# PEER feed-forward on one core: constants, index lists and gated Gelu values kept in PSUM as one operand of VectorE's steps, and one step per half for the index products

## The chip, the cores and the metric

One core of a Trainium2 chip runs the whole program in one launch. The time is the device time of that core in microseconds; the kernel before was run three times, and the median stands for it. Five engines matter: TensorE (PE, with its weight loads PEld), VectorE (DVE), ScalarE (ACT), GpSimd (POOL) and the queue of SyncE (SP), which issues the large transfers. Tiles lie in SBUF or in PSUM; in this kernel PE's results go to PSUM, and POOL's steps have all their operands in SBUF.

## The reference

A model of two blocks on 512 tokens of width 1024: gated linear attention, a convolutional feed-forward, grouped-query attention, the feed-forward again; then a mixer of an mLSTM and stick-breaking attention, a cross attention over 256 memory tokens, and PEER, a feed-forward that looks its experts up. PEER is all that the change touches:

```python
q = (xt @ wq).reshape(T, 8, 2, 128)                  # 8 heads, two halves of a product key
s = einsum('thpc,hpnc->thpn', q, subkeys)            # 128 sub-keys per half
s_top, i_top = top_k(s, 16)
cand = s_top[:, :, 0, :, None] + s_top[:, :, 1, None, :]
cand_idx = i_top[:, :, 0, :, None] * 128 + i_top[:, :, 1, None, :]
best, pos = top_k(cand.reshape(T, 8, 256), 16)
experts = take_along_axis(cand_idx.reshape(T, 8, 256), pos)
gates = softmax(best)
act = gelu(einsum('cd,ced->ce', x, u[experts])) * gates
y = einsum('ce,ced->cd', act, v[experts])            # 128 experts a token, of 16384
```

## The kernel before, in words

All matrix products run in three passes of rounded high and low parts (`mm3`, L188 to L190), so each operand is split: ACT rounds the high part, DVE or POOL subtracts it (for weights L115 and L118, where `lsplit` says which engine makes which tile's low part).

`peer` (from L1148) works in four stages.

- Projections: 16 query tiles. DVE takes the top 16 of each list (`top16`, L1179 to L1183). On the way the normalised tokens 128 to 511 are scaled (`xf`, L1209) and split (`xnh` by ACT, `xnl` by POOL, L1212).
- Routing, `route(t)` for 128 tokens (order 1, 2, 3, then 0): best 16 of 60 candidate sums per head, then per half a comparison of 128x2048 with the 16-element iota (L1279), eight products with the index list `tf`, one per head (L1282; POOL takes heads 1 and 5, DVE the six others), and a reduction (L1286). For tokens 0 to 127 the result is the index column `idx` (L1359).
- One-hots, `onehots(t)` for tokens 128 to 511: 32 steps of 4 tokens. Each makes two one-hot tiles by comparing with the 128-element iota `iot` in SBUF: the first on DVE (L1321) or, every third step, on POOL (L1319); the second on DVE with its gate (L1332), or on DVE and ACT (L1325, L1330). PE multiplies them into an `ax` PSUM tile (L1334), ACT moves it to `stage` (L1336). The stages of tokens 128 to 383 are flushed to DRAM (`Gd`, 16 transfers of 1 MB on SP), that of the last 128 tokens stays. Meanwhile `fill` makes 42 of the 128 "up" products ahead of time and stores their Gelu values in DRAM (`Hd`).
- The gate stretch: all 16384 experts densely for tokens 128 to 511, in 128 tiles of 128 experts. A list `mix` strings 86 fresh and 42 stored tiles evenly, so that two fresh ones are mostly followed by a stored one. For each tile `gate(j)` has Gelu values (fresh: 24 matmuls, Gelu by ACT at L1229 from PSUM to the SBUF tile `gel`; stored: `gst`, fetched), multiplies them by the gate matrix (DVE L1450 with the fetched `gm`, 128x256; L1451 with `stage`, 128x128), and splits them (`ah` by ACT L1454, `al` by DVE L1455). `down()` runs one tile behind: 18 matmuls of 512 columns with the "pv" weights into six PSUM tiles `Y`, which stay for the whole stretch. In the same stretch tokens 0 to 127 are done expert by expert: POOL gathers rows of u and v (L1411), DVE makes the dot product (L1419), ACT its Gelu (L1420), DVE multiplies by the gate (L1427) and adds the v row (L1428).

PSUM has eight tiles of 128x512: four named `mm`, four `ax`. A scheduler sets each engine's order from the program's dependencies; where two steps touch one tile, the order of the program holds.

## Time and profile before

| | |
|---|---|
| median of three runs | 3059.61 us (3058.24 to 3059.70) |
| span of the profiled execution | 3059.2 us, 0.4 under that median |
| PE busy | 2939.6 us (96%) |
| DVE busy | 2103.6 us (69%) |
| ACT, POOL busy | 1324.5 us (43%), 1237.5 us (40%) |
| PE's granted clock, mean | 0.990 |
| share of the span by what ended the chain of waits | PE 22%, DVE 5%, ACT 2%, DMA 1%; the rest shows no wait |

Busy time is the union of an engine's instructions; PE's matmuls overlap in the record, so a busy PE is one with work in it, and what it loses is read from its idle time and from the waits. PEER starts near 1660 us: projections until 1780, routing and one-hots until 2120, the gate stretch until 3052.

### The profile page before, as it was taken

How to read it: one execution, taken by the hardware profiler on the slowest of the kernel's cores; microseconds unless marked ns; L12 is line 12 of the kernel's file. 1: busy time of each engine (PE TensorE's matmuls, PEld its weight loads, DVE VectorE, ACT ScalarE, POOL GpSimd, SP SyncE). 2: the span in 40 equal slices, each digit the busy share in tenths (PEclk: the TensorE clock that was granted, in tenths of full speed). 3: DMA queues.
4: the chain of work that ended last, by engine and by line, in shares of the span. 5: the costliest groups of instructions: out<-in, count | busy, mean ns of one | idle time of the engine just before them, and what ended most of it. 6: DMA issues, size and time to landing. Idle time of an engine off the chain costs nothing. (4 is left out here: it accounts for less than half of the span.)

```text
span 3059.2 us, 38865 instructions
## 1 busy us (share of the span) xinstructions
PE 2939.6 (96%) x14251; PEld 2460.2 (80%) x14251; DVE 2103.6 (69%) x3665; ACT 1324.5 (43%) x2174; POOL 1237.5 (40%) x773
## 2 busy tenths in 40 slices
PE   8999999999999999999999989789999999999998
PEld 6778888788788887875888778788888888888887
DVE  4656554557664546448645789985888878888786
ACT  4454333356542335326444346655333333333333
POOL 3224322342332323105313446755555555555453
PEclk9999999999999999999999989999999999999999
DMA  4113333321223332321332335374888888888785
GB/s 137 58 49 104 95 92 97 103 91 35 76 90 97 97 97 91 97 62 35 109 98 80 93 103 159 114 221 168 285 299 300 297 300 297 306 294 289 286 293 191
DMA packets 166095, 472.90 MB, mean 155 GB/s; under 512 B 15368, under 2 KB 79240, under 8 KB 149520
## 3 DMA queue, kind: packets, MB, share of 16 engines
q1 hardware_dynamic: 135840, 322.73, 33.5%
q0 software_dynamic: 18432, 134.23, 11.2%
q10 hardware_dynamic: 11632, 13.46, 1.3%
q8 instruction: 112, 1.84, 0.2%
q14 instruction: 79, 0.65, 0.1%
HBM read 443.23 MB, written 27.13 MB: 154 GB/s over the span
## 5 line engine op out<-in xcount | busy, mean ns | idle before, releaser
L118 POOL TENSOR_TENSOR wl<-w,wh 128x1024 fp32r<-128x1024 f32 x242 | 611.1, 2526 | 903.6 <-ACT wh L115 778.8
L115 ACT ACTIVATE wh<-w 128x1024 fp32r<-128x1024 f32 (+1 forms) x530 | 559.1, 1055 | 794.3 <-PE mm L189 500.6
L188 PE MATMUL mm<-sh,wh 128*128 128x512 f32 (+1 forms) x1888 | 752.2, 399 | 8.3 <-ACT sh L219 6.7
L189 PE MATMUL mm<-sl,wh 128*128 128x512 f32 (+1 forms) x1888 | 750.9, 398 | 2.3 <-POOL sl L199 1.3
L190 PE MATMUL mm<-sh,wl 128*128 128x512 f32 (+1 forms) x1888 | 748.6, 397 | 0.2 <-DVE wl L118 0.2
L118 DVE TENSOR_TENSOR wl<-w,wh 128x1024 fp32r<-128x1024 f32 (+1 forms) x288 | 366.2, 1272 | 229.7 <-ACT wh L115 222.5
L188 PEld LDWEIGHTS mm<-sh,wh 128*128 128x128 f32 (+1 forms) x1888 | 354.7, 188 | 97.1 <-ACT sh L219 7.2
L189 PEld LDWEIGHTS mm<-sl,wh 128*128 128x128 f32 (+1 forms) x1888 | 354.6, 188 | 92.1 <-issue 3.6
L190 PEld LDWEIGHTS mm<-sh,wl 128*128 128x128 f32 (+1 forms) x1888 | 354.8, 188 | 85.2 <-issue 1.4
L188 PE MATMUL mm<-xnh,wh 128*128 128x384 f32 x1024 | 348.3, 340 | 1.4 <-ACT gel L1229 1.4
L190 PE MATMUL mm<-xnh,wl 128*128 128x384 f32 x1024 | 347.3, 339 | 1.6 <-DVE wl L118 1.6
L189 PE MATMUL mm<-xnl,wh 128*128 128x384 f32 x1024 | 346.1, 338 | 0.0
L188 PEld LDWEIGHTS mm<-xnh,wh 128*128 128x128 f32 x1024 | 194.0, 189 | 5.1 <-ACT gel L1229 1.7
L189 PEld LDWEIGHTS mm<-xnl,wh 128*128 128x128 f32 x1024 | 194.0, 189 | 3.3
L190 PEld LDWEIGHTS mm<-xnh,wl 128*128 128x128 f32 x1024 | 193.9, 189 | 2.6 <-DVE wl L118 2.5
L188 PE MATMUL mm<-wh,ah 128*128 128x512 f32 x384 | 154.2, 402 | 35.8 <-ACT ah L1454 35.8
L279 DVE TENSOR_TENSOR xT<-xT,mm 128x512 f32<-128x512 f32 x80 | 54.7, 686 | 171.8 <-PE mm L190 171.8
L190 PE MATMUL mm<-wh,al 128*128 128x512 f32 x384 | 154.1, 401 | 2.3 <-DVE al L1455 2.3
L1411 POOL DMA_INDIRECT xT<-in_uv_dram,idx x64 | 101.6, 1588 | 129.3 <-DVE xt L1428 80.1
L189 PE MATMUL mm<-wl,ah 128*128 128x512 f32 x384 | 152.4, 397 | 0.0
L1411 POOL DMA_INDIRECT uv<-in_uv_dram,idx x64 | 101.0, 1578 | 126.0 <-DVE xt L1428 79.0
L189 PE MATMUL ax<-wl,ah 128*128 128x512 f32 x384 | 150.3, 391 | 0.0
(452 smaller groups left out, 5110.3 us busy)
## 6 DMA issues: line engine op xcount, KB each, us to landing
w<-in_pu_dram SPq DMA_DIRECT2D x128, 512.0 KB, 4.5
w<-in_pv_dram SPq DMA_DIRECT2D x128, 512.0 KB, 4.0
w<-in_up_dram SPq DMA_DIRECT2D x88, 512.0 KB, 3.5
w<-in_down_dram SPq DMA_DIRECT2D x48, 512.0 KB, 3.5
Gd<-stage SPq DMA_DIRECT2D x16, 1024.0 KB, 8.8
gm<-Gd SPq DMA_DIRECT2D x128, 128.0 KB, 5.4
w<-in_pq_dram SPq DMA_DIRECT2D x16, 512.0 KB, 3.6
Hd<-gel ACTq DMA_DIRECT2D x42, 192.0 KB, 1.9
```

Of the source, the lines that this page charges most:

```text
L115: SC.activation(h[:, :n], w[:, :n], AF.Copy)
L118: ins = eng.tensor_tensor(l[:, :n], w[:, :n], h[:, :n].bitcast(F32), ALU.subtract)
L188: PE.matmul(ps, lhsT=lh, rhs=rh, start=start, stop=False)
L189: PE.matmul(ps, lhsT=lh, rhs=rl, start=False, stop=False)
L190: PE.matmul(ps, lhsT=ll, rhs=rh, start=False, stop=stop)
L279: V.tensor_tensor(xT[:, c], xT[:, c], ps, ALU.add)
L1411: G.indirect_dma_start(out=uv, out_offset=None, in_=A["uv"], in_offset=bass.IndirectOffsetOnAxis(ap=idx[:, k:k + 1], axis=0))
```

## The change

- `norm.finish(in_psum=True)` leaves the norm factor of PEER in its PSUM tile; `xf` is an `ax` PSUM tile, and its low part is made by DVE instead of POOL.
- One `ax` tile `cst` is taken for routing and one-hots. ACT copies both iotas into it, and `route` writes its index list into its other half (L1248). The comparisons of DVE (L1284, L1325, L1329, L1336) and the index products read it there. POOL's own one-hots still read `iot` in SBUF.
- The eight index products of a half are one DVE step (L1287).
- Gelu values of the gate stretch stay in PSUM: `gate(j)` takes in turn an `mm` and an `ax` tile (`Y` holds three of each), Gelu works in place, a stored tile is copied into it by ACT (L1459), DVE multiplies in place (L1460, L1461), and ACT and DVE split it from there (L1464, L1465).
- The dot's value is multiplied by its gate on ACT (`SC.activation(d, d, AF.Copy, scale=...)`) instead of on DVE.

```diff
-        def finish(self, bc=True, col=False):
+        def finish(self, bc=True, col=False, in_psum=False):
-                self.rstd = main.tile([P, S], F32, name="rstd", tag="rstd", bufs=1)[:, :n]
+                self.rstd = ps if in_psum else main.tile([P, S], F32, name="rstd", tag="rstd", bufs=1)[:, :n]
...
-                xf = q_("xf", (P, TD), bufs=2)
+                xf = axps()[:, :TD]
-                G.tensor_tensor(xnl[:, c], xf, xnh[:, c].bitcast(F32), ALU.subtract)
+                V.tensor_tensor(xnl[:, c], xf, xnh[:, c].bitcast(F32), ALU.subtract)
...
+        cst = axps()
+        SC.activation(cst[:, 0:P], iot, AF.Copy)
+        SC.activation(cst[:, P:P + 16], iota, AF.Copy)
+        iotp, iotap, tfp = cst[:, 0:P], cst[:, P:P + 16], cst[:, 256:512]
...
-            tf = r_("tf", (P, 16, 16))
-            V.tensor_copy(tf, ti[t])
+            V.tensor_copy(tfp.rearrange("p (a b) -> p a b", b=16), ti[t])
+            tf = tfp.rearrange("p (h f k) -> p h f k", f=2, k=16)
...
-                for h in range(8):
-                    (G if h % 4 == 1 else V).tensor_tensor(oh[:, h * 16:(h + 1) * 16], oh[:, h * 16:(h + 1) * 16],
-                                    tf[:, 2 * h + half].rearrange("p (o i) -> p o i", o=1)
-                                    .to_broadcast([P, 16, 16]), ALU.mult)
+                o4 = oh.rearrange("p (h k) i -> p h k i", k=16)
+                V.tensor_tensor(o4, o4, tf[:, :, half].rearrange("p h (o i) -> p h o i", o=1)
+                                .to_broadcast([P, 8, 16, 16]), ALU.mult)
...
-            io4 = iot.rearrange("p (o i) -> p o i", o=1).to_broadcast([P, 4, P])
+            io4 = iotp.rearrange("p (o i) -> p o i", o=1).to_broadcast([P, 4, P])
...
-                        V.tensor_scalar(oh2[:, k], iot, rt[:, 1, tk:tk + 1], rt[:, 2, tk:tk + 1],
+                        V.tensor_scalar(oh2[:, k], iotp, rt[:, 1, tk:tk + 1], rt[:, 2, tk:tk + 1],
...
             SC.activation(d, d, AF.Gelu)
+            SC.activation(d, d, AF.Copy, scale=gate0[:, k:k + 1])
...
-                V.tensor_tensor(d, d, gate0[:, k:k + 1], ALU.mult)
...
-            gm, g = fetched.pop(j)
-            if g is None:
-                g = up(j)
+            gm, st = fetched.pop(j)
+            g = (mmps, axps)[turn[0] % 2]()[:, :TD]
+            turn[0] += 1
+            if st is None:
+                up(j, g)
+                SC.activation(g, g, AF.Gelu)
+            else:
+                SC.activation(g, st, AF.Copy)
             V.tensor_tensor(g[:, :2 * P], g[:, :2 * P], gm, ALU.mult)
```

How the order of DVE's instructions moves is seen at two places. The first is the end of routing. Before, the last part of `route(0)` stands between two one-hot stages: the index products (`oh` with `tf`), the reductions `e0` and `e1` and `idx` come ahead of the first comparisons of the last one-hots (`oh1`, `oh2`).

```order
L1279 TENSOR_TENSOR oh_17195<-fj_17165,iota_12802 128x2048
L1294 RECIPROCAL sm_17209<-sm_17209 128x8
L1282 TENSOR_TENSOR oh_17195<-oh_17195,tf_17113 128x256 x6
L1295 TENSOR_TENSOR gate0_12797<-gate0_12797,sm_17209 128x128
L1286 TENSOR_REDUCE e1_17205<-oh_17195 128x128
L118 TENSOR_TENSOR wl_16105<-w_15996,wh_16104 128x1024
L1358 SCALAR_TENSOR_TENSOR e0_17193<-e0_17193,e1_17205 128x128
L1359 CAST idx_12796<-e0_17193 128x128
L118 TENSOR_TENSOR wl_16175<-w_16066,wh_16174 128x1024
L1321 TENSOR_TENSOR oh1_16349<-rt_16345,iot_12804 128x512
L1325 TENSOR_TENSOR oh2_16351<-rt_16345,iot_12804 128x512
```

With the change they follow the last one-hots, directly ahead of the first tile's gate products; `ax_13859` is `cst`.

```order
L1329 TENSOR_TENSOR oh2_16972<-rt_16302,ax_13859 128x512
L1336 TENSOR_SCALAR oh2_16990<-ax_13859,rt_16302 128x128 x4
L1248 CAST ax_13859<-ti0_12810 128x256
L1284 TENSOR_TENSOR oh_17139<-fi_17120,ax_13859 128x2048
L1287 TENSOR_TENSOR oh_17139<-oh_17139,ax_13859 128x2048
L1290 TENSOR_REDUCE e0_17142<-oh_17139 128x128
L118 TENSOR_TENSOR wl_17232<-w_16906,wh_17231 128x1024
L1284 TENSOR_TENSOR oh_17144<-fj_17121,ax_13859 128x2048
L1287 TENSOR_TENSOR oh_17144<-oh_17144,ax_13859 128x2048
L1290 TENSOR_REDUCE e1_17147<-oh_17144 128x128
L1362 SCALAR_TENSOR_TENSOR e0_17142<-e0_17142,e1_17147 128x128
L1363 CAST idx_12796<-e0_17142 128x128
```

Moved are the write of the index list (L1248) and all that reads it, behind the last step that compares with `cst`. The lists of tokens 256 to 511 are written behind the one-hots of the tokens before them in the same way.

The second place is in the gate stretch, a fresh tile followed by a stored one. Before (`gel` fresh, `gst` stored, `scr` and `xt0` the dot step of tokens 0 to 127, `wl` a weight's low part):

```order
L118 TENSOR_TENSOR wl_20679<-w_20530,wh_20678 128x1024
L1450 TENSOR_TENSOR gel_20707<-gel_20707,gm_20561 128x256
L1451 TENSOR_TENSOR gel_20707<-gel_20707,stage_16348 128x128
L1455 TENSOR_TENSOR al_20712<-gel_20707,ah_20711 128x384
L1419 SCALAR_TENSOR_TENSOR scr_20740,dot_20739<-xT_67,xn_17240 128x1024
L1427 TENSOR_TENSOR dot_20667<-dot_20667,gate0_12797 128x1
L1455 TENSOR_TENSOR al_20751<-gst_20602,ah_20750 128x384
L1428 SCALAR_TENSOR_TENSOR xt0_17227<-uv1_17273,dot_20667,xt0_17227 128x1024
L118 TENSOR_TENSOR wl_20757<-w_20604,wh_20756 128x1024
```

With the change (`mm` the fresh tile, `ax` the stored one):

```order
L118 TENSOR_TENSOR wl_20474<-w_20327,wh_20473 128x1024
L1460 TENSOR_TENSOR mm_20433<-mm_20433,gm_20317 128x256
L1461 TENSOR_TENSOR mm_20433<-mm_20433,stage_16305 128x128
L1465 TENSOR_TENSOR al_20468<-mm_20433,ah_20467 128x384
L1423 SCALAR_TENSOR_TENSOR scr_20496,dot_20495<-xT_67,xn_17182 128x1024
L1432 SCALAR_TENSOR_TENSOR xt0_17169<-xT_67,dot_20424,xt0_17169 128x1024
L1465 TENSOR_TENSOR al_20509<-ax_20504,ah_20508 128x384
L1423 SCALAR_TENSOR_TENSOR scr_20537,dot_20536<-uv0_17214,xn_17182 128x1024
L1432 SCALAR_TENSOR_TENSOR xt0_17169<-xT_67,dot_20495,xt0_17169 128x1024
L118 TENSOR_TENSOR wl_20551<-w_20400,wh_20550 128x1024
```

The sequence is the same around the gate products; the step L1427 is gone from DVE, and in place of `gel` and `gst` the operands are `mm` and `ax`, that is, PSUM.

## Rows read from the trace of the kernel before

**Rows 1.** Busy time by stage: us, busy us of each engine (instructions), granted clock, DMA share, GB/s:

```profile
1660.00:1780.00 120.00, 118.10 (x580) 96.54 (x579) 89.94 (x524) 44.48 (x68) 51.12 (x27) 1.00 0.31 87
1780.00:2120.00 340.00, 291.52 (x1831) 278.95 (x1830) 296.23 (x785) 207.84 (x427) 209.38 (x182) 0.94 0.48 148
2120.00:3052.00 932.00, 893.67 (x4342) 786.02 (x4341) 769.72 (x1007) 334.88 (x570) 479.90 (x232) 0.99 0.80 288
```

**Rows 2.** Waits, 2110 to 3060: engine, tile and line, releaser, us, times, longest:

```profile
PE mm L188 <- ACT ah L1454: 35.8, 24, 3.7
...
PE mm L190 <- DVE al L1455: 2.3, 1, 2.3
```

**Rows 3.** Timeline of DVE: start, us, instruction, idle before it:

```profile
2432.19 3.22 DVE L1450 TENSOR_TENSOR gel<-gel,gm 128x256 f32<-128x256 f32 x1 [0.31 <-ACT gel L1229]
2435.34 0.28 DVE L1451 TENSOR_TENSOR gel<-gel,stage 128x128 f32<-128x128 f32 x1
```

**Rows 4.** Timeline of POOL, the same stretch:

```profile
2431.02 1.69 POOL L1411 DMA_INDIRECT xT<-in_uv_dram,idx  x1 [4.51 <-PE mm L190]
2432.73 2.40 POOL L118 TENSOR_TENSOR wl<-w,wh 128x1024 fp32r<-128x1024 f32 x1
```

**Rows 5.** Timeline of ACT, the same stretch:

```profile
2431.69 0.47 ACT L1229 ACTIVATE gel<-mm 128x384 f32<-128x384 f32 x1
2435.71 0.52 ACT L1454 ACTIVATE ah<-gel 128x384 fp32r<-128x384 f32 x1 [3.55 <-DVE gel L1451]
```

**Rows 6.** Timeline of PE, the same stretch:

```profile
2436.29 0.51 PE L188 MATMUL mm<-wh,ah 128*128 128x512 f32 x1 [1.38 <-ACT ah L1454]
```

**Rows 7.** Lines L1450, L1451: duration ns least/median/most, first and last start:

```profile
L1450 DVE TENSOR_TENSOR gel<-gel,gm x86: 412/420/3241, 2119.5 to 3041.1; 128x256 f32<-128x256 f32 x86
L1451 DVE TENSOR_TENSOR gel<-gel,stage x86: 275/283/3167, 2121.7 to 3041.4; 128x128 f32<-128x128 f32 x86
```

**Rows 8.** Line L279:

```profile
L279 DVE TENSOR_TENSOR xT<-xT,mm x80: 674/687/690, 227.1 to 1664.3; 128x512 f32<-128x512 f32 x80
```

**Rows 9.** Groups by line and shape, 1660 to 2120: busy us, mean ns, idle before:

```profile
L1332 DVE TENSOR_SCALAR oh<-iot,rt 128x128 f32<-128x128 f32 x252 | 84.6, 395 | 4.0 <-PE ax L1334 4.0
...
L1321 DVE TENSOR_TENSOR oh<-rt,iot 128x512 f32<-128x512 f32 x63 | 51.8, 822 | 20.0 <-ACT rt L1305 10.1 <-PE ax L1334 9.7
...
L1282 DVE TENSOR_TENSOR oh<-oh,tf 128x256 f32<-128x256 f32 x48 | 34.1, 745 | 0.0
L1325 DVE TENSOR_TENSOR oh<-rt,iot 128x512 f32<-128x512 f32 x33 | 27.8, 842 | 0.0
...
L1279 DVE TENSOR_TENSOR oh<-fj,iota 128x2048 f32<-128x2048 f32 x4 | 9.1, 2285 | 0.0
```

**Rows 10.** Lines L1332, L1321, L1282: ns least/median/most:

```profile
L1332 DVE TENSOR_SCALAR oh<-iot,rt x252: 329/336/2422, 1818.9 to 2097.1; 128x128 f32<-128x128 f32 x126
L1321 DVE TENSOR_TENSOR oh<-rt,iot x63: 668/679/2876, 1817.7 to 2093.1; 128x512 f32<-128x512 f32 x63
L1282 DVE TENSOR_TENSOR oh<-oh,tf x48: 405/415/2630, 1797.0 to 2016.3; 128x256 f32<-128x256 f32 x48
```

**Rows 11.** Lines L888 (source in PSUM) and L1264 (in SBUF):

```profile
L888 DVE TENSOR_SCALAR W<-ax,colt x16: 342/343/351, 1292.4 to 1368.6; 128x128 f32<-128x128 f32 x16
L1264 DVE TENSOR_SCALAR pi<-bi x8: 215/219/315, 1790.3 to 1995.3; 128x128 uint32<-128x128 uint32 x8
```

**Rows 12.** Busy time in pieces: flush gaps, one-hots, the seam behind them:

```profile
1880.00:1930.00 50.00, 39.73 (x229) 39.05 (x227) 48.80 (x130) 20.41 (x27) 26.04 (x17) 0.96 0.95 293
1930.00:1995.00 65.00, 56.38 (x366) 52.21 (x367) 63.62 (x191) 50.06 (x116) 47.60 (x46) 0.93 0.19 60
1995.00:2033.00 38.00, 36.99 (x213) 36.33 (x212) 28.77 (x38) 16.08 (x22) 13.90 (x9) 1.00 1.04 308
2033.00:2100.00 67.00, 57.28 (x387) 54.31 (x388) 56.28 (x117) 51.97 (x119) 50.85 (x51) 0.95 0.34 110
2100.00:2120.00 20.00, 18.60 (x128) 18.25 (x127) 4.34 (x5) 7.06 (x11) 8.02 (x5) 1.00 0.62 202
```

More of the change, by code (lines that the diff above doesn't have):

```diff
@@ L1194, in peer @@
             if i == 0:
-                norm.finish(bc=True, col=True)
+                norm.finish(bc=True, col=True, in_psum=True)
                 V.tensor_copy(rcol, norm.col)
@@ L1220, in peer, with up @@
         hp = rctx.enter_context(tc.tile_pool(name="hp", bufs=1, side="right", reuse_waits="tile"))
-        def up(j):
+        def up(j, ps):
             uh, ul = weight("pu", j)
-            ps = mmps()[:, :TD]
             for c in range(8):
@@ L1227, in up, with up_store @@
                 mm3(ps, uh[:, s], ul[:, s], xnh[:, c], xnl[:, c], c == 0, c == 7)
+        def up_store(j):
+            ps = mmps()[:, :TD]
+            up(j, ps)
             g = hp.tile([P, TD], F32, name="gel", tag="gel", bufs=3)
             SC.activation(g, ps, AF.Gelu)
-            return g
-        def up_store(j):
-            nc.scalar.dma_start(Hd[j], up(j))
+            nc.scalar.dma_start(Hd[j], g)
         ahead = deque(range(NA))
@@ L1279, in route @@
                 V.tensor_tensor(oh, pf.rearrange("p h (k o) -> p (h k) o", o=1).to_broadcast([P, P, 16]),
-                                iota.rearrange("p (o i) -> p o i", o=1).to_broadcast([P, P, 16]), ALU.is_equal)
-                for h in range(8):
-                    (G if h % 4 == 1 else V).tensor_tensor(oh[:, h * 16:(h + 1) * 16], oh[:, h * 16:(h + 1) * 16],
-                                    tf[:, 2 * h + half].rearrange("p (o i) -> p o i", o=1)
-                                    .to_broadcast([P, 16, 16]), ALU.mult)
+                                iotap.rearrange("p (o i) -> p o i", o=1).to_broadcast([P, P, 16]), ALU.is_equal)
+                o4 = oh.rearrange("p (h k) i -> p h k i", k=16)
+                V.tensor_tensor(o4, o4, tf[:, :, half].rearrange("p h (o i) -> p h o i", o=1)
+                                .to_broadcast([P, 8, 16, 16]), ALU.mult)
                 e = r_(f"e{half}", (P, P), bufs=2)
@@ L1435, in peer @@
         fetched = {}
+        turn = [0]
         def fetch(j):
```

## Prediction

> **What bounds the kernel now.** I read the busy table by stage first [rows 1]. TensorE (PE) is the bound nearly everywhere, but not equally. While the product-key queries are projected (1660 to 1780 us) it is busy 118.1 of 120 us: nothing that the change does there can show. While lists are routed and one-hots are built (1780 to 2120) it is busy 291.5 of 340 us and VectorE (DVE) 296.2: 48 us of PE's time stand open, and DVE is the fuller engine. In the gate stretch (2120 to 3052) PE is busy 893.7 of 932 us, DVE 769.7: 38 us stand open. These two stretches are all that the change can win from.
>
> Next come the waits of the gate stretch. PE's idle time has one name: 35.8 us in 24 waits of the first product for `ah`, and 2.3 us for `al` [rows 2]. To see what is late I follow one of them in the order of time. ScalarE (ACT) starts Gelu at 2431.69 [rows 5], DVE starts the product with `gm` (L1450) at 2432.19, and that step, of 128x256, takes 3.22 us [rows 3], where its median is 0.420 [rows 7]. Meanwhile GpSimd (POOL) gathers until 2432.71 and then splits a weight until 2435.13 [rows 4]; DVE's step ends 0.3 us after that. `ah` starts at 2435.71 [rows 5], PE at 2436.29 after 1.38 us idle [rows 6]. So a DVE step whose two inputs lie in SBUF, started beside a POOL step, lasts until POOL is done. Both gate products show it in their maxima: 3.24 us against 0.41, and 3.17 against 0.28 [rows 7]. The counter-example is L279, which adds a PSUM tile to an SBUF tile: all 80 lie between 0.674 and 0.690 us [rows 8], though POOL splits weights in that part of the program as well.
>
> The Trainium skill says the same (SBUF — State Buffer, section Who interferes with whom): VectorE with two SBUF inputs shares a read port with a GpSimd instruction that reads SBUF, the second to issue is blocked for the whole of the first, and with at most one SBUF input there is no contention outside the doubled modes. The 3.22 us and L279's narrow spread agree with it.
>
> **The change, part by part.**
>
> *Gate values in PSUM.* The two gate products get one PSUM input and one SBUF input; so does the subtraction that makes `al`. If L279 is the pattern, the 3 us cases go. What then remains of a gate: Gelu begins at 2431.69 and PE could have taken the product at 2436.29 - 1.38 = 2434.91, so 3.2 us are there. The undisturbed chain is about 0.5 (Gelu, from 2431.69 to 2432.19) + 0.42 + 0.28 + the hand-over to `ah` and from `ah` to PE, 0.09 + 0.58 (2435.62 to 2435.71, and on to 2436.29): 1.9 us, slack 1.3. The second product now waits for the first one; before, its start overlapped the end of the first by 0.07 [rows 3], and a hand-over is 0.09, so some 0.15 us per tile, inside the slack. ACT copies 42 stored tiles into PSUM: some 0.5 us each, 21 us on an engine that is busy 335 of 932 us [rows 1]; such a copy waits until a tile's buffer comes free, and a weight split queued behind it on ACT waits too, by less than a DVE step. Multiplying the dot value by its gate goes from DVE to ACT, 128 one-column steps; neither engine is the bound. No row shows DVE or ACT writing PSUM. Bounds: from nothing to what would use up the 1.3 us; I take nothing: L279 reads PSUM and shows no wait [rows 8], and it is the nearest row. Of the 38.1 us I take 36 as gone, with 2 left to starts of stretches. Ends: 20 (if every second POOL step now catches another DVE step that stands ahead of a gate) and 42 (matmuls also restart slowly after each of the 24 waits: 0.51 us in the row of rows 6).
>
> *One step for index products.* Per half, six DVE steps and two POOL steps become one DVE step of 128x2048. DVE's 48 steps are 34.1 us of busy time [rows 9], their mean 0.745 us against a median of 0.415 [rows 10]: POOL's own two stand beside them. The new step's nearest row is L1279, 128x2048, 2.28 us [rows 9]: 8 x 2.28 = 18.3. DVE saves 15.9 us, three quarters of it, 12, in the routes of tokens 128 to 511, which lie on the path; route(0) is seen below.
>
> *Constants in PSUM.* L1321 and L1325 compare two SBUF operands: 63 at a mean of 0.822 and 33 at 0.842 us [rows 9] against a median of 0.679 [rows 10]: 96 x 0.15 = 14 us of waiting for POOL's own one-hots, which goes. L1332 has one tensor operand: mean 0.395 [rows 9], median 0.336 [rows 10], so 252 x 0.059 = 15 us to win. Against it stands the price of PSUM as the source: L888, a 128x128 step of the same kind out of PSUM, takes 0.343 us, while L1264 out of SBUF takes 0.219 [rows 11]. So L1332 lands between 0.343 (+2 us over the 252) and 0.336 + 0.124 = 0.46 (+31); I take the middle, 0.40, +16, because L888 carries one pointer and L1332 two. Net 0; ends -13 and +16.
>
> The Trainium skill has a rule that speaks against this part (VectorE: DVE Perf Modes, section Why PSUM operands drop a tier): a one-source 32-bit step runs at double rate only out of SBUF. By that rule the 252 steps would be slower than now and the middle value would be right; by L888 alone, whose 0.343 is close to 0.336, the sum would be 13 us better.
>
> *What it does to the path.* DVE is busy 48.8 of 50, 63.6 of 65 and 56.3 of 67 us in the pieces where I say that it decides [rows 12], so 12 + 14 = 26 us less DVE work shortens the stretch by as much, if nothing else is late next. Two things could be. PE is busy 56.4 of 65 and 57.3 of 67 in the one-hot pieces [rows 12], so such a piece can shrink by 9 at most, three of them by 27 if the first is like the others. And the 16 flushes keep the DMA engines full, 0.95 and 1.04 of their time, in both gaps [rows 12]; a stage tile cannot be overwritten before its flush is read. In the second gap DVE already idles (28.8 of 38): there is nothing to win there, and the moved products of route(3), which now follow the one-hots of the tile before, find room. I take 26; ends +10 and -45 (all 48 us of PE's open time but 3).
>
> *What moves.* Index lists and iota lie in one tile, so a list can only be written after the one-hots that read that tile. For route(0) this puts six passes of 128x2048 (13.7 us) behind the last one-hots instead of into the flush gap. There, 2100 to 2120, DVE is busy 4.3 us and PE 18.6 with stored tiles and transposes [rows 12]: PE covers them. If it did not, up to 14 us come back. One of four `ax` buffers is pinned, leaving three for one-hot products; ACT empties one while PE fills another, so I cost it at nothing; without that cover, it is in the +10.
>
> *Projection stage.* Eight subtractions move from POOL to DVE, which is busy 89.9 of 120 us while PE is full [rows 1]: nothing.
>
> **Sum.** The profiled span is 3059.2 us, 0.4 below the median of the runs, 3059.6. 0 - 26 - 36 = -62: **2998 us** by the median. 0.2%, 6 us, is about what a measurement here can tell from no change.
>
> **The rivals.** (1) *Only the gate stretch gains.* The flush gaps and PE's own work set the one-hot stretch, DVE only fills time. For it: DMA at 0.95 to 1.04 in the gaps; against it: DVE idles for 1.2 and 1.4 us only in two of the pieces [rows 12]. 3059.6 - 36 = 3024.
>
> (2) *The block moves to a neighbour.* A weight split on DVE (L118) and the dot step after the gate still have two SBUF inputs, and stand before the next gate in DVE's queue; DVE had only 0.31 us to spare before the gate [rows 3]. A POOL step of 2.4 us that meets such a neighbour delays the gate by up to 2.1. If that keeps half of the waits: 3059.6 - 18 - 26 = 3016.
>
> The Trainium skill's page SBUF — State Buffer, in the same section, gives this rival its reason: what counts is who issues first, not which step it is.
>
> (3) *The change does not do what it says*: steps in place in PSUM are stretched beside POOL as before, because the other operand still comes from SBUF. Then only the joined index products win, and the moved ones give some back: 3059.6 - 12 + 12 = 3060. L279's spread speaks against it.
>
> (4) *Slower.* Writing PSUM is dear, the one price that no row shows. Gelu, both products and the stored copies write PSUM. From 1.3 us extra per gate on, the second of each pair of fresh tiles (43 of them) holds PE up; at 2.7 us extra the 62 us are eaten up (43 x 1.4 = 60), and at 3.4 us the kernel ends at 2998 + 43 x 2.1 = 3088. It would need these steps, 1.2 us together, to take nearly four times as long.
>
> **How the numbers follow.** Forecast 0.57; rival 1 0.13; rival 2 0.15; rival 3 0.05; rival 4 0.07; 0.03 for a loss by several small things at the seams. Faster by over 0.2%: 0.86 (the first three, with a hundredth for mixtures); within 0.2%: 0.05; slower: 0.09. The range takes in the forecast's bounds (route stretch -45, gate stretch -42, not both in full) and reaches past rivals 1 and 2: 2968 to 3042.
>
> **What would show it.** After the change the maxima of both gate products (L1460, L1461) should lie under 0.6 us, and PE's waits for `ah` in the gate stretch be under 6 us in all. The one-hot comparisons L1325 and L1329 should have means within 3% of their medians; L1336 shows the price of PSUM as source: near 0.34 or near 0.40. L1287 should take about 2.3 us. The one-hot pieces should be near 57 us each, PE-bound. It is wrong if the dot steps, L118 or the 3.2 us cases stand right ahead of late gates (rival 2), if the flush gaps have not moved while DVE idles more (rival 1), or if Gelu into PSUM takes well over 0.5 us (rival 4).

## The result, and the profile after

| | before | with the change |
|---|---|---|
| median | 3058.93 us (3055.99 to 3059.70) | 2979.97 us (2974.41 to 2980.35) |
| ratio | | 0.9739, 95% interval 0.9725 to 0.9752 |
| span of the profiled execution | 3059.2 us | 2972.1 us |

The change made the kernel 79 us faster; 62 were forecast, and the time lies inside the range. The profiled execution of the changed kernel was its fastest (2974.41 us), so the two profiles lie 87 us apart, 8 more than the medians. One profiled execution, that of e6 below, ran at a mean granted clock of 0.566 and took 4709 us, so e6 is given by the median of its four others and has no profile here. For a table by stage I cut both at the same marks: the last query product (L1201), the first `al` of the gate stretch, and the last output step. First and last starts are in these rows of single lines, of the kernel before

```profile
L1201 PE MATMUL ax<-sk,q x128: 270/275/377, 1672.2 to 1774.8; 128*128 128x128 f32 x128
L1455 DVE TENSOR_TENSOR al<-gel,ah x86: 557/558/2967, 2122.6 to 3042.4; 128x384 fp32r<-128x384 f32 x86
L1386 DVE SCALAR_TENSOR_TENSOR uv<-ax,fst,fb x3: 740/743/751, 3050.7 to 3054.7; 128x512 f32<-128x512 f32 x3
```

and of the changed one:

```profile
L1201 PE MATMUL ax<-sk,q x128: 272/275/377, 1669.4 to 1769.7; 128*128 128x128 f32 x128
L1465 DVE TENSOR_TENSOR al<-mm,ah x64: 543/557/559, 2083.8 to 2949.3; 128x384 fp32r<-128x384 f32 x64
L1390 DVE SCALAR_TENSOR_TENSOR uv<-ax,fst,fb x3: 740/743/749, 2963.6 to 2967.6; 128x512 f32<-128x512 f32 x3
```

| stage | before | with the change | difference | forecast |
|---|---|---|---|---|
| to the last query product | 1774.8 | 1769.7 | -5.1 | 0 |
| routing and one-hots, to the first `al` | 347.8 | 314.1 | -33.7 | -26 |
| gate stretch, to the last output | 932.1 | 883.8 | -48.3 | -36 |

Of the 5.1, 2.7 lie ahead of the projections, where nothing was changed, and 2.4 in them (e7). Both other stages gave more than forecast, in about the same proportion. A few of the 33.7 may be scatter: the profiles of e1, e10 and e11, whose routing and one-hots are the changed kernel's, have 315.5 to 318.6 us for it.

The stage that lost 33.7 us can be cut further, at the first and the last one-hot product of each 128 tokens (PE's L1334, with the change L1338). The "flush gaps" are the two pieces between the one-hots of two token tiles:

| piece | before | with the change |
|---|---|---|
| last query product to first one-hot | 45.2 | 41.6 |
| one-hots, tokens 128 to 255 | 59.5 | 55.7 |
| first flush gap | 51.3 | 36.9 |
| one-hots, tokens 256 to 383 | 63.9 | 59.1 |
| second flush gap | 42.0 | 43.0 |
| one-hots, tokens 384 to 511 | 62.4 | 57.7 |
| seam, to the first `al` | 23.5 | 20.0 |

The first flush gap alone gave 14.4 us, the three one-hot pieces 13.3 together. Busy time in the two flush gaps, columns as in [rows 1], before

```profile
1879.50:1930.80 51.30, 40.25 (x233) 39.58 (x232) 50.10 (x134) 21.08 (x29) 26.84 (x18) 0.95 0.93 287
1994.70:2036.70 42.00, 37.29 (x215) 36.62 (x214) 32.74 (x44) 16.50 (x24) 17.60 (x11) 0.98 1.05 311
```

and with the change:

```profile
1867.10:1904.00 36.90, 31.49 (x169) 30.32 (x168) 33.08 (x103) 13.14 (x22) 7.95 (x7) 0.91 1.02 306
1963.00:2006.10 43.10, 37.08 (x213) 35.78 (x211) 40.60 (x135) 20.31 (x29) 13.04 (x9) 0.98 1.03 313
```

Part of a route moved from the first gap, where DVE was full, to the second, where it had idled. Before, the last route for the one-hots (`route(3)`) made its list at 1900.8 us and its first reduction at 1923.8, in the first gap; with the change its list is written at 1961.6, behind the one-hots that read `cst`, and both its reductions end by 1987.5, in the second gap.

In the gate stretch the signs asked for are there. The gate products, formerly [rows 7], in the rows of their lines (least/median/most, ns):

```profile
L1460 DVE TENSOR_TENSOR mm<-mm,gm x64: 418/426/433, 2079.6 to 2941.1; 128x256 f32<-128x256 f32 x64
L1460 DVE TENSOR_TENSOR ax<-ax,gm x64: 418/425/433, 2084.2 to 2953.9; 128x256 f32<-128x256 f32 x64
L1461 DVE TENSOR_TENSOR mm<-mm,stage x64: 298/299/300, 2080.1 to 2941.5; 128x128 f32<-128x128 f32 x64
```

The longest of 128 is 0.433 us where it was 3.241. All waits of PE of the gate stretch by tile and line, from 2070 on, formerly [rows 2]:

```profile
PE mm L190 <- DVE al L1465: 2.6, 1, 2.6
PE ax L1405 <- ACT xt L1399: 1.9, 1, 1.9
PE mm L188 <- ACT ah L1464: 1.7, 2, 1.0
```

24 waits for `ah` of 35.8 us have become two of 1.7. The same situation as in [rows 3 to 6], a weight split on POOL beside a gate product, now reads so, in the timelines of POOL and of DVE:

```profile
2412.13 2.40 POOL L118 TENSOR_TENSOR wl<-w,wh 128x1024 fp32r<-128x1024 f32 x1 [0.44 <-ACT wh L115]
```

```profile
2412.46 0.43 DVE L1460 TENSOR_TENSOR mm<-mm,gm 128x256 f32<-128x256 f32 x1 [1.59 <-ACT mm L1457]
2412.93 0.30 DVE L1461 TENSOR_TENSOR mm<-mm,stage 128x128 f32<-128x128 f32 x1
2413.85 0.56 DVE L1465 TENSOR_TENSOR al<-mm,ah 128x384 fp32r<-128x384 f32 x1 [0.62 <-ACT ah L1464]
```

All three DVE steps run inside POOL's 2.40 us, none longer than elsewhere. The rows of the routing and one-hot stage, formerly [rows 9, 10], by line:

```profile
L1325 DVE TENSOR_TENSOR oh<-rt,ax x63: 671/686/690, 1809.5 to 2058.7; 128x512 f32<-128x512 f32 x63
L1329 DVE TENSOR_TENSOR oh<-rt,ax x33: 674/680/683, 1810.1 to 2059.3; 128x512 f32<-128x512 f32 x33
L1336 DVE TENSOR_SCALAR oh<-ax,rt x252: 396/401/411, 1810.7 to 2060.9; 128x128 f32<-128x128 f32 x126
L1287 DVE TENSOR_TENSOR oh<-oh,ax x8: 2267/2275/2287, 1793.3 to 2073.2; 128x2048 f32<-128x2048 f32 x8
```

No comparison is stretched any more, and the one-hot pieces of 55.7, 59.1 and 57.7 us lie near the 57 that were named as a sign. The scalar step pays for PSUM as its source, 0.401 against a median of 0.336 [rows 10], and the single index step takes 2.28 us, both as forecast. Busy time in the stages of the changed kernel:

```profile
1769.60:2079.60 310.00, 286.54 (x1852) 275.39 (x1850) 271.35 (x770) 206.91 (x429) 156.69 (x165) 0.97 0.51 159
2079.60:2964.00 884.40, 879.52 (x4347) 785.74 (x4348) 631.28 (x883) 387.99 (x741) 459.64 (x233) 1.00 0.82 305
```

PE stands idle for 5 us of the gate stretch where it was 38 [rows 1], and DVE is 138 us less busy.

### The profile page after: what moved, and what is told of

Its sections match the earlier page's. It is cut to its first block, busy times and chain, and to the rows that moved or that the text cites. A ratio compares the mean times of both kernels' runs of the same rounds, so it can differ in the third digit from the quotient of the medians.

```text
span 2972.1 us, 38991 instructions
## 1 busy us (share of the span) xinstructions
PE 2914.9 (98%) x14251; PEld 2451.1 (82%) x14251; DVE 1935.5 (65%) x3505; ACT 1374.1 (46%) x2346; POOL 1157.5 (39%) x749
## 4 chain that ended last, share of the span: by engine, by line
PE 87%; DVE 5%; ACT 3%; issue 2%; DMA 1%; POOL 1%; SPq 0%; ACTq 0%; DVEq 0%; POOLq 0%
PE mm L188 21%; PE mm L189 21%; PE mm L190 21%; PE ax L188 5%; PE ax L189 5%; PE ax L190 5%; PE ax L1338 2%; ACT wh L115 1%; DMA w<-in_pu_dram 1%; ACT stage L1340 1%; PE mm L1021 1%; PE ax L1201 1%; PE ax L991 0%; DVE wl L118 0%; PE ax L447 0%
## 5 line engine op out<-in xcount | busy, mean ns | idle before, releaser
L118 POOL TENSOR_TENSOR wl<-w,wh 128x1024 fp32r<-128x1024 f32 x242 | 618.5, 2556 | 1064.1 <-ACT wh L115 924.1
L118 DVE TENSOR_TENSOR wl<-w,wh 128x1024 fp32r<-128x1024 f32 (+1 forms) x288 | 368.6, 1280 | 282.0 <-ACT wh L115 275.6
L190 PE MATMUL mm<-xnh,wl 128*128 128x384 f32 x688 | 236.6, 344 | 4.1 <-POOL wl L118 3.5
L188 PE MATMUL mm<-xnh,wh 128*128 128x384 f32 x688 | 236.8, 344 | 3.6 <-ACT wh L115 3.6
L189 PE MATMUL mm<-xnl,wh 128*128 128x384 f32 x688 | 236.0, 343 | 0.0
L279 DVE TENSOR_TENSOR xT<-xT,mm 128x512 f32<-128x512 f32 x80 | 54.7, 686 | 171.7 <-PE mm L190 171.7
L188 PE MATMUL ax<-wh,ah 128*128 128x512 f32 x384 | 149.8, 390 | 0.0
L190 PE MATMUL ax<-wh,al 128*128 128x512 f32 x384 | 149.4, 389 | 0.0
L555 POOL TENSOR_TENSOR y<-y 128x512 f32<-128x512 f32 x44 | 56.8, 1292 | 228.8 <-ACT y L554 228.8
L547 DVE SCALAR_TENSOR_TENSOR y<-u,vecs,y 128x512 f32<-128x512 f32 x88 | 113.8, 1293 | 42.0 <-ACT y L546 42.0
L188 PEld LDWEIGHTS mm<-xnh,wh 128*128 128x128 f32 x688 | 130.9, 190 | 6.0 <-ACT wh L115 4.2
```

The source lines that it names most:

```text
L118: ins = eng.tensor_tensor(l[:, :n], w[:, :n], h[:, :n].bitcast(F32), ALU.subtract)
L188: PE.matmul(ps, lhsT=lh, rhs=rh, start=start, stop=False)
L189: PE.matmul(ps, lhsT=lh, rhs=rl, start=False, stop=False)
L190: PE.matmul(ps, lhsT=ll, rhs=rh, start=False, stop=stop)
L279: V.tensor_tensor(xT[:, c], xT[:, c], ps, ALU.add)
L547: V.scalar_tensor_tensor(y, u[:, 0:S], w[0], y, op0=ALU.mult, op1=ALU.add)
```

## The experiments

All are the changed kernel or the kernel before with one part altered. Stages are cut at the marks above.

| kernel | median us | routing, one-hots | gate stretch |
|---|---|---|---|
| before | 3058.93 | 347.8 | 932.1 |
| changed | 2979.97 | 314.1 | 883.8 |
| e1, gate values in SBUF | 3015.67 | 318.0 | 920.0 |
| e2, gate values in PSUM only | 3008.96 | 345.9 | 883.6 |
| e3, before, POOL splits nothing | 3007.96 | 348.9 | 880.3 |
| e4, iotas in SBUF | 2996.81 | 333.6 | 885.3 |
| e5, scalar step from SBUF | 2984.49 | 321.0 | 883.7 |
| e6, eight index steps | 2985.54 | | |
| e7, projection as before | 2981.58 | 314.9 | 886.2 |
| e8, lists apart | 2979.13 | 314.4 | 883.8 |
| e9, before, POOL splits all | 3221.88 | 341.4 | 1097.9 |
| e10, changed, POOL splits all | 3032.89 | 318.6 | 940.0 |
| e11, changed, POOL splits nothing | 2978.64 | 315.5 | 883.3 |
| e12, e8 and e11 together | 2980.25 | 317.9 | 883.7 |

e1 to e4, e5 to e8 and e9 to e12 ran with the kernel before beside them, whose medians were 3058.2, 3057.2 and 3057.27.

**e1.** Gate values back in SBUF.

```diff
-            g = (mmps, axps)[turn[0] % 2]()[:, :TD]
-            turn[0] += 1
+            g = st
             if st is None:
-                up(j, g)
-                SC.activation(g, g, AF.Gelu)
-            else:
-                SC.activation(g, st, AF.Copy)
+                ps = (mmps, axps)[turn[0] % 2]()[:, :TD]
+                turn[0] += 1
+                up(j, ps)
+                g = hp.tile([P, TD], F32, name="gel", tag="gel", bufs=3)
+                SC.activation(g, ps, AF.Gelu)
```

> The changed kernel with one part undone: Gelu writes an SBUF tile again and stored values are used from SBUF, while the two PSUM tiles still take turns for the fresh products and the dot's gate stays on ACT. Theory A (a DVE step with two SBUF inputs lasts until the POOL step beside it is done): both gate products have maxima near 3.2 us again, PE's waits for ah in the gate stretch are over 30 us, the time is 2980 + 47 = about 3027 us. Rival B (the gate stretch won by the two PSUM tiles taking turns and by the step that left DVE): the time stays within 10 us of 2980 and the waits under 10 us.

3015.67 us, 36 more than the change. The waits and the line's row are back:

```profile
PE mm L188 <- ACT ah L1464: 24.9, 23, 2.7
```

```profile
L1460 DVE TENSOR_TENSOR gel<-gel,gm x86: 410/420/3155, 2083.9 to 2995.5; 128x256 f32<-128x256 f32 x86
```

Rival B falls: two PSUM tiles in turn and one DVE step less don't prevent the waits. 24.9 us of them in 23 cases are fewer than 35.8 in 24, and fewer than the 30 that were expected, so the size, 47, was too large; the 11 us between may belong to these two parts when the operand lies in SBUF, which no run separates.

**e2.** The kernel before with the PSUM part of `gate(j)` alone (the split of `up` into `up` and `up_store` that goes with it is left out here).

```diff
-            gm, g = fetched.pop(j)
-            if g is None:
-                g = up(j)
+            gm, st = fetched.pop(j)
+            g = (mmps, axps)[turn[0] % 2]()[:, :TD]
+            turn[0] += 1
+            if st is None:
+                up(j, g)
+                SC.activation(g, g, AF.Gelu)
+            else:
+                SC.activation(g, st, AF.Copy)
```

> The kernel before with only the gate values moved to PSUM (the dot's gate stays on DVE, routing and one-hots as before). Theory A: maxima of the gate products under 0.6 us, PE's waits for ah under 6 us, the gate stretch 47 us shorter, 3059 - 47 = 3012 us. Rival C (the gate stretch needs the dot's gate off DVE too): 3025 us or more.

PE's waits for `ah` are 4.4 us in three cases, and the gate products are short:

```profile
PE mm L188 <- ACT ah L1460: 4.4, 3, 2.8
```

```profile
L1456 DVE TENSOR_TENSOR ax<-ax,gm x64: 415/425/433, 2108.0 to 2987.1; 128x256 f32<-128x256 f32 x64
```

3008.96 us. The gate stretch is 883.6 us as in the changed kernel: gate values in PSUM, with the two tiles in turn that hold them, give the whole 48, and moving the dot's gate to ACT adds nothing. Rival C falls.

**e3.** Nothing in PSUM; POOL only gathers in the gate stretch.

```diff
-        lsplit[:] = [V, G]
+        lsplit[:] = [V]
```

> The kernel before, all operands in SBUF, but in the gate stretch DVE makes every low part of the weights; POOL only gathers. That gives DVE about 106 x 1.22 = 129 us more of its own work. Theory A: long gate products are left only beside gathers, PE's waits for ah fall from 36 to 10 to 20 us, 3059 - 20 = 3039 us (3020 to 3050). Rival B, or any theory by which DVE's amount of work sets the gate: the fuller DVE makes the waits longer, 3060 us or more.

3007.96 us, under the 3020 to 3050 that I expected: the gate stretch is 880.3, no longer than with PSUM operands, and DVE did the 106 splits besides, some 129 us at 1.22 each. The row of the first gate product, and of the gathers that ran beside it:

```profile
L1450 DVE TENSOR_TENSOR gel<-gel,gm x86: 416/418/421, 2121.0 to 2988.9; 128x256 f32<-128x256 f32 x86
```

```profile
L1411 POOL DMA_INDIRECT uv<-in_uv_dram,idx x64: 937/1677/3818, 2105.2 to 2966.1; - x64
```

So in this stretch the gathers hold nothing up; the weight splits did it all. This corrects my reading of [rows 4]. Counting, over the timelines of the gate stretch, which steps of DVE overlap which of POOL:

| DVE step | beside nothing | beside a gather alone | beside a split |
|---|---|---|---|
| L1450, before | 46: 0.41 to 0.43 | 50: 0.41 to 0.43 | 29: 2.47 to 3.24 |
| L1460, changed | 44: 0.42 to 0.43 | 24: 0.42 | 59: 0.42 to 0.43 |
| L118, e3 | 85: 1.21 to 1.23 | 124: 1.21 to 1.23 | none |
| dot step L1419, before | 81: 1.21 to 1.23 | 42: 1.21 to 1.22 | 5: 1.22 to 1.23 |
| dot step L1423, changed | 62: 1.21 to 1.22 | 4: 1.21 | 62: 1.22 to 3.43, 20 of them over 2.9 |
| v-row step L1428, before | 50: 1.27 to 1.29 | 21: 1.27 to 1.28 | 57: 1.27 to 3.43, 20 of them over 2.9 |
| v-row step L1432, changed | 43: 1.27 to 1.28 | 22: 1.27 to 1.28 | 63: 1.27 to 3.41, 2 of them over 2.9 |

(A step that meets a gather and a split stands under the split.)

The last four rows show what became of the rest. The dot step, which still has two SBUF inputs, is stretched 20 times instead of never, but in place of the step that adds the v row, which was stretched 20 times before and is now twice. In the rows of the two lines (least/median/most, ns), before and with the change:

```profile
L1428 DVE SCALAR_TENSOR_TENSOR xt<-uv,dot,xt x64: 1270/1284/3426, 2159.2 to 3038.6; 128x1024 f32<-128x1024 f32 x64
```

```profile
L1432 DVE SCALAR_TENSOR_TENSOR xt<-uv,dot,xt x64: 1272/1275/2962, 2117.5 to 2949.8; 128x1024 f32<-128x1024 f32 x64
```

So the stretching of the gate products did not move elsewhere. What all DVE steps of the stretch took beyond their usual durations sums to some 191 us before, 43 with the change, and nothing in e3.

**e4.** The iotas back in SBUF; the list and the single index step stay.

```diff
-        SC.activation(cst[:, 0:P], iot, AF.Copy)
-        SC.activation(cst[:, P:P + 16], iota, AF.Copy)
-        iotp, iotap, tfp = cst[:, 0:P], cst[:, P:P + 16], cst[:, 256:512]
+        iotp, iotap, tfp = iot, iota, cst[:, 256:512]
```

> The changed kernel with both iotas read from SBUF again; the index list stays in PSUM, its product stays one step. Theory A: the one-hot comparisons have means near 0.82 us again with a median of 0.68, the tensor-scalar step is back at a median of 0.336 with maxima over 2 us, and the routing and one-hot stretch is 10 to 20 us longer: about 2995 us. Rival D (that stretch won by the single index step, the constants did nothing): within 4 us of 2980.

2996.81 us, 16.8 more by the medians; routing and one-hots are 19.5 longer in the profile. The groups by line, 1600 to 2130:

```profile
L1323 DVE TENSOR_TENSOR oh<-rt,iot 128x512 f32<-128x512 f32 x63 | 56.1, 891 | 23.2 <-PE ax L1336 13.0 <-ACT rt L1307 10.1
L1327 DVE TENSOR_TENSOR oh<-rt,iot 128x512 f32<-128x512 f32 x33 | 27.1, 820 | 0.0
```

Theory A holds and rival D falls: means of 0.891 and 0.820 against 0.682 and 0.680 in the changed kernel make 63 x 0.209 + 33 x 0.140 = 18 us. In this kernel the order also lets routes run ahead again, so not every one of the 19.5 is the operand's: 12.7 lie in the three one-hot pieces, but 5.2 in the first flush gap, where `route(3)` has its list and a reduction again.

**e5.** The scalar step alone reads SBUF again.

```diff
-                        V.tensor_scalar(oh2[:, k], iotp, rt[:, 1, tk:tk + 1], rt[:, 2, tk:tk + 1],
+                        V.tensor_scalar(oh2[:, k], iot, rt[:, 1, tk:tk + 1], rt[:, 2, tk:tk + 1],
```

> The changed kernel, but the one-hot step with two scalars (L1336, 252 of them) reads iota from SBUF again; the 128x512 comparisons still read PSUM. Theory A with its price of PSUM as the source: the step's median is back at 0.336 us from 0.401, which saves 16 us of DVE's work, and its maxima are back over 2 us, which gives about as much away: within 5 us of 2980. Rival E (the slower rate is the only effect on this step): 10 us or more below 2980.

2984.49 us, 4.5 more; its interval (0.9747 to 0.9784) overlaps the changed kernel's.

```profile
L1336 DVE TENSOR_SCALAR oh<-iot,rt 128x128 f32<-128x128 f32 x252 | 98.2, 449 | 1.6 <-PE ax L1338 1.6
```

Rival E falls. The step's median is 0.336 again but its mean 0.449, more than the 0.401 out of PSUM: what PSUM costs in rate it gives back in steps that POOL no longer stretches.

**e6.** Eight index steps per half, two on POOL, lists in an SBUF tile.

```diff
-            V.tensor_copy(tfp.rearrange("p (a b) -> p a b", b=16), ti[t])
-            tf = tfp.rearrange("p (h f k) -> p h f k", f=2, k=16)
+            tfs = r_("tf", (P, 256))
+            V.tensor_copy(tfs.rearrange("p (a b) -> p a b", b=16), ti[t])
+            tf = tfs.rearrange("p (h f k) -> p h f k", f=2, k=16)
...
-                o4 = oh.rearrange("p (h k) i -> p h k i", k=16)
-                V.tensor_tensor(o4, o4, tf[:, :, half].rearrange("p h (o i) -> p h o i", o=1)
-                                .to_broadcast([P, 8, 16, 16]), ALU.mult)
+                for h in range(8):
+                    (G if h % 4 == 1 else V).tensor_tensor(oh[:, h * 16:(h + 1) * 16], oh[:, h * 16:(h + 1) * 16],
+                                    tf[:, h, half].rearrange("p (o i) -> p o i", o=1)
+                                    .to_broadcast([P, 16, 16]), ALU.mult)
```

> The changed kernel with the index products as before: eight steps per half, two of them on POOL, lists in an SBUF tile. Theory A: DVE's six have a mean near 0.7 us again, some 13 us more of DVE's time on the routes of tokens 128 to 511, 2987 to 2995 us. Rival G (the index products are covered by PE's stored tiles): within 4 us of 2980.

2985.54 us, 5.6 more: less than theory A's 7 to 15, more than rival G's 4. The single step, with its lists in PSUM, is worth about 6 us, hardly clear of the noise: the interval (0.9747 to 0.9780) just meets the changed kernel's.

**e7.** The projection stage as before.

```diff
-                norm.finish(bc=True, col=True, in_psum=True)
+                norm.finish(bc=True, col=True)
...
-                xf = axps()[:, :TD]
+                xf = q_("xf", (P, TD), bufs=2)
...
-                V.tensor_tensor(xnl[:, c], xf, xnh[:, c].bitcast(F32), ALU.subtract)
+                G.tensor_tensor(xnl[:, c], xf, xnh[:, c].bitcast(F32), ALU.subtract)
```

> The changed kernel with the projection stage as before: norm factor and xf in SBUF, the low part subtracted by POOL. In the profiles this stage is 2.4 us shorter with the change (104.2 and 101.8). Theory A: PE is full there, so the 2.4 us are PE's waits behind stretched steps and return: 2982 us. Rival: no difference that can be measured, and the stage stays at 102 us.

2981.58 us, within the interval of the changed kernel. From the first query copy to the last query product its profile has 104.1 us, like the kernel before with 104.2, where the changed kernel has 101.8: the 2.4 us return, but the time cannot tell them from nothing. In the profiles they are real: this stretch has 101.8 to 101.9 us in the eight with the changed stage and 104.1 to 104.3 in the five with the old one. They are waits of PE, as theory A has it. In e7, from 1663 to 1772, and in the same words in the kernel before, there is this one, and none with the change:

```profile
PE ax L1201 <- ACT q L1198: 1.9, 2, 1.5
```

**e8.** Index lists and the 16-element iota in a PSUM tile of their own.

```diff
-        SC.activation(cst[:, P:P + 16], iota, AF.Copy)
-        iotp, iotap, tfp = cst[:, 0:P], cst[:, P:P + 16], cst[:, 256:512]
+        cst2 = mmps()
+        SC.activation(cst2[:, P:P + 16], iota, AF.Copy)
+        iotp, iotap, tfp = cst[:, 0:P], cst2[:, P:P + 16], cst2[:, 256:512]
```

> The changed kernel with the index lists and the 16-element iota in a PSUM tile of their own (an mm tile), apart from the 128-element iota. In the order of instructions half of route(0)'s products then come ahead of the last one-hots. Theory A, as forecast: PE has enough stored tiles at the seam, so nothing is won, 2978 to 2982 us. Rival F (products that share the tile cost time at the seam or in the flush gaps): 2966 to 2975 us.

2979.13 us: nothing is won, as forecast. The stretch from the last one-hot product to the first `al` is 15.0 us instead of 20.0, and that from the last flush to the last one-hot product 74.6 instead of 69.3: the products of route(0) cost the same on either side. In the order of instructions only half of them moved, and those of tokens 256 to 511 stayed behind the one-hots, so the shared tile was not the whole reason for their place.

**e9.** The suspected cost doubled in the kernel before.

```diff
-        lsplit[:] = [V, G]
+        lsplit[:] = [G]
```

> The kernel before, all operands in SBUF, but in the gate stretch POOL makes every low part (212 steps of about 2.5 us instead of 106). The suspected cost doubled. Theory A: about twice as many gate products are stretched, PE's waits for ah rise from 36 to 55 to 90 us, 3059 + 35 = 3094 us (3075 to 3130). Rival (what delays the gates is DVE's amount of work): DVE loses 129 us of its own, the waits fall, 3040 us or less. Rival (POOL too full for the weights): PE waits for low parts (wl) instead of ah.

3221.88 us, ratio 1.0544 (1.0526 to 1.0561): the right direction, but 163 us instead of 35. PE has no wait for `wl`, so the last rival falls. It waits for `al` and `ah`:

```profile
PE mm L190 <- DVE al L1455: 120.5, 41, 6.7
...
PE mm L188 <- ACT ah L1454: 29.8, 21, 4.9
```

The timelines of DVE and POOL show why each case is longer:

```profile
2551.91 5.37 DVE L1450 TENSOR_TENSOR gel<-gel,gm 128x256 f32<-128x256 f32 x1 [0.74 <-ACT gel L1229]
```

```profile
2551.24 0.94 POOL L1411 DMA_INDIRECT uv<-in_uv_dram,idx  x1 [1.05 <-DVE gst L1451]
2552.20 4.79 POOL L118 TENSOR_TENSOR wl<-w,wh 128x1024 fp32r<-128x1024 f32 x2
```

Two splits follow each other without a gap, and DVE's step lasts until the second is done. Most of the loss stands before `al`, whose subtraction also has two SBUF inputs here. DVE had less work of its own than before and PE waited four times as long, so it is not the amount of DVE's work that delays the gates.

The waits are not all of the loss. They grew by 112 us, from 38 to 150. Busy time in the gate stretch of e9, columns as in [rows 1]:

```profile
2117.70:3215.60 1097.90, 946.98 (x4337) 816.99 (x4337) 868.58 (x903) 339.66 (x575) 686.20 (x337) 0.93 0.70 245
```

The granted clock is 0.93 in the mean, where it was 0.99 before [rows 1]: the trace has 24 spells at the lower level, 0.50 of full speed or 1.2 GHz, 157 us together, each at one of PE's waits. Matmuls in these spells start some 45 us later than at full clock, gaps of over 0.3 us left out, against 5.5 us in the kernel before. So about 40 of the 163 us go with the clock.

**e10.** The same edit as e9, in the changed kernel.

> The changed kernel with the same doubling: POOL makes every low part in the gate stretch. Theory A: gate products have one operand in PSUM and stay under 0.45 us, PE's waits for ah stay under 6 us; POOL has 212 x 2.5 + 128 x 1.6 = 735 us of work in 884, so weights may come late now and then: 2980 to 2995 us, 100 us under the kernel before with the same doubling. Rival (the change only made room on DVE): the waits for ah come back, 3010 us or more.

3032.89 us: 189 under e9, but 53 over the changed kernel. Theory A's time fails. The time and the returning waits are those named for the rival, but not its reason: here DVE has less work of its own than in the changed kernel, and the waits come back all the same. The gate products hold (the first row), the dot steps don't (groups by line, the second fence), and PE waits for `ah` again (the third):

```profile
L1460 DVE TENSOR_TENSOR mm<-mm,gm x64: 418/432/433, 2090.9 to 3006.9; 128x256 f32<-128x256 f32 x64
```

```profile
L1423 DVE SCALAR_TENSOR_TENSOR scr<-xT,xn 128x1024 f32<-128x1024 f32 x64 | 224.4, 3507 | 5.0 <-DMA xT<-in_uv_dram,idx 5.0
```

```profile
PE mm L188 <- ACT ah L1464: 37.7, 31, 4.3
```

The timelines of DVE and POOL for one of them:

```profile
2578.25 6.87 DVE L1423 SCALAR_TENSOR_TENSOR scr<-xT,xn 128x1024 f32<-128x1024 f32 x1
...
2586.25 0.42 DVE L1460 TENSOR_TENSOR mm<-mm,gm 128x256 f32<-128x256 f32 x1
```

```profile
2576.89 7.15 POOL L118 TENSOR_TENSOR wl<-w,wh 128x1024 fp32r<-128x1024 f32 x3
```

The dot step is held through what is left of three splits in a row, and the gate product, two places behind it on DVE (the v-row step stands between), starts at 2586.25 without any idle time before it: ACT had copied its stored tile by 2578.87, so it was ready and queued. That is rival 2 of the prediction, at work once POOL has twice the splits. In the changed kernel itself it is there in small, though not by the dot step: neither of the two waits, 1.7 us together, stands behind a stretched one. Ahead of the first is a weight split on DVE, which takes 1.22 us elsewhere:

```profile
2316.09 2.54 DVE L118 TENSOR_TENSOR wl<-w,wh 128x1024 fp32r<-128x1024 f32 x1
```

The second follows the last v-row step of tokens 0 to 127 (2.96 us), whose end the final norm on ACT awaits, with a Gelu queued behind it.

**e11, e12.** The edit of e3 in the changed kernel (e11), and together with that of e8 (e12).

> The changed kernel with every low part of the gate stretch on DVE, none on POOL. Theory A: the gate stretch has 6 us left over PE's own work, most of it at its first tile, so at most 3 us are won: 2975 to 2981 us. Rival (dot steps and weight splits that POOL still stretches hold gates up): 2970 us or less. If DVE becomes too full, 2985 us or more.

> The changed kernel with lists apart from the 128-element iota and no weight split on POOL in the gate stretch: the two variants that could beat it, together. Theory A: both are at what PE needs, 2972 to 2980 us. More than 10 us below 2980 would say that a wait is left that the profile of the changed kernel does not show.

2978.64 (0.9728 to 0.9761) and 2980.25 us (0.9727 to 0.9760): no difference from the changed kernel, though e12 lies a quarter of a microsecond over the range expected for it. The last 1.7 us of waits are too few to matter, and no version beat the changed kernel by more than its interval.

## Why the prediction was right, and where its sizes were off

- *PE's open time lies in two stages, and DVE's stretched steps cause the gate waits.* Right, by e1, e2, e3 and e9: take away the SBUF operand or POOL's split, and the waits go; double the splits, and PE waits four times as long.
- *"A DVE step whose two inputs lie in SBUF, started beside a POOL step, lasts until POOL is done."* Too wide. In the gate stretch only the weight splits do it; gathers like that of [rows 4] ran beside 50 gate products of 0.41 to 0.43 us. The Trainium skill (SBUF — State Buffer, Who interferes with whom) names GpSimd instructions that read SBUF, and the weight splits agree with it. That the block lasts for the whole of "the first" is not all: in e9 and e10 DVE stood behind two and three splits in a row. Nor does the record show which came first: 28 of the 29 stretched gate products start 0.10 to 0.55 us ahead of their split by the record, as in [rows 3, 4] (2432.19 and 2432.73), and all 29 end 0.29 or 0.30 us behind its end. Why a step that takes 0.42 us alone is not done by then stays open.
- *Gate stretch, -36.* It was -48.3. The term that was too small is what a wait costs besides its idle time, which I left to the upper bound. Summing, over the matmuls of the stretch, the distance from start to start beyond the undisturbed 0.2275 us (512 columns) and 0.1735 us (384 columns): 54.5 us before, 6.4 with the change. Of the 48 that went, 37.6 stood in gaps of over 0.3 us and 10.4 in smaller ones, nearly all within 15 us behind such a gap. The smaller ones are of two kinds, about half each. One is the first matmuls behind a wait. The timeline of PE in the kernel before, behind the wait of [rows 6]:

```profile
2436.63 0.40 PE L189 MATMUL mm<-wl,ah 128*128 128x512 f32 x1
2436.88 0.50 PE L190 MATMUL mm<-wh,al 128*128 128x512 f32 x1
2437.21 0.39 PE L188 MATMUL mm<-wh,ah 128*128 128x512 f32 x1
```

  The first matmul after the wait holds the second up by 0.34 us, the third holds the fourth by 0.33, against 0.2275. The wait was entered as 1.38 us; with its start and these it cost about 1.8. The other kind is the clock, a term that the prediction does not have. Before, the stretch has three spells at the lower level, 13.7 us together, each at a wait of 2.3 to 3.7 us; with the change it has none (1.00 in the last row of the result). One of them, busy time with the granted clock in the third column from the end, and two matmuls in it:

```profile
2253.20:2256.60 3.40, 3.40 (x10) 2.55 (x9) 3.40 (x7) 1.09 (x2) 0.13 (x1) 0.50 0.91 353
```

```profile
2254.39 0.63 PE L189 MATMUL mm<-wl,ah 128*128 128x512 f32 x1
2254.82 0.63 PE L190 MATMUL mm<-wh,al 128*128 128x512 f32 x1
```

  They start 0.43 us apart instead of 0.2275. The three spells cost 5.5 us in such distances.
- *Writing PSUM costs nothing.* Right, the one price that no row had shown: 0.426 against 0.420 us for the first product, 0.299 against 0.283 for the second, and Gelu in place 0.475 us in the row below, where it took 0.47 into SBUF [rows 5]. Rival 4 falls.

```profile
L1457 ACT ACTIVATE mm<-mm x44: 469/475/476, 2079.1 to 2935.6; 128x384 f32<-128x384 f32 x44
```

- *Constants in PSUM, 14 us from the comparisons and 0 net from the scalar step.* 17 to 19.5 by e4, which undoes both and lets `route(3)` run ahead again; 0 to 5 for the scalar step by e5. The step's price was 0.401 against 0.336 us. That 0.40 met it so well is luck: it was the middle of two bounds, and the reason given for it, one pointer against two, was not tested. By the Trainium skill's rule a PSUM operand loses the doubled rate (VectorE: DVE Perf Modes, Why PSUM operands drop a tier). The trace agrees in direction; with one length of step, 128 elements, no run tells a lower rate from a longer start.
- *One index step, 12 us on the path.* About 6 by e6.
- *Routing and one-hots, -26 in all.* It was -33.7. Undone one at a time, the parts give 17 to 19.5 and about 6; some 8 to 11 us belong to no part alone. The prediction entered only what moved products might cost, and put at nothing what DVE saves where they leave: the first flush gap, which it took for DVE's (48.8 of 50 us busy), lost work of `route(3)` and gave 14.4 us, while the second, where it saw room, grew by 1.0. No run undoes the move alone, so its share stays open; so does that of the clock, 0.94 in this stage before [rows 1] and 0.97 with the change.
- *Moved index products cost nothing at the seam.* Right, by e8, though the reason given for their place, the shared tile, is only part of it.
- *Projection stage, nothing.* PE was not quite full there: two waits for `q`, and 2.4 us in the profiles, not to be told apart in the time (e7).
- *Rival 1* is refuted by the stage table, *rival 3* by the rows of L1460 and L1461. *Rival 2* is real but was small, 0.7 us behind one weight split on DVE: to matter it needs more POOL work than this kernel has (e10).

## What to carry to other kernels

When a short VectorE step shows a maximum many times its median, look at what GpSimd does at that moment: if the step has two SBUF inputs and GpSimd runs a tensor step on SBUF operands, as the weight splits here, either put one operand in PSUM (e2, 49 us) or give GpSimd's step to VectorE if that has the room (e3, 50 us). The two cure the same thing and do not add up (e11). Cure the step that another engine waits for, and check what stands ahead of it in the queue with two SBUF inputs, since that can hold it up in turn (e10).

## What the runs showed that I had not expected

- Indirect gathers on POOL did not stretch any two-input step of DVE: 124 weight splits on DVE beside gathers in e3 took 1.21 to 1.23 us, as long as alone.
- A held DVE step is not let in between two POOL steps that follow without a gap: 5.37 us behind two, 6.87 behind three.
- The loss grows much faster than POOL's work: twice the splits cost the kernel before 163 us more (e9), where the first half had cost about 50 (e3). DVE's steps were stretched about in proportion, by some 412 us in all against 191; it is PE's waits that rose fourfold, and the clock came on top.
